# Modulation rows of a conditioned transformer block: outputs on partitions, contraction along the free axis

## The chip, the cores and the metric

One core of a Trainium2 chip runs the whole program. The metric is the device time of one execution in microseconds (us). TensorE (PE) multiplies matrices, VectorE (DVE), ScalarE (ACT) and GpSimd (POOL) work on 128 partitions of SBUF, and SyncE (SP) and ACT issue the transfers (DMAs) from DRAM.

## What is computed

A model of three blocks, all in float32, on 256 tokens of width 1024. Layers 0 and 1 are alike: a mixer (attention within a band, a short convolution, two sigmoid gates), then a gated feed-forward part of width 2816. The third block ("block 2") has a mixer of stick-breaking attention and pooling and a feed-forward part, and its norms and residual gates are modulated by six rows of 1024 numbers, which depend on nothing but a vector `c`:

```python
mod = jax.nn.silu(c) @ w_cond[l] + b_cond[l]          # (1, 1024) @ (1024, 6144)
shift_m, scale_m, gate_m, shift_f, scale_f, gate_f = jnp.split(mod, 6, axis=-1)
h = rmsnorm(x, g_mix_pre[l]) * (1.0 + scale_m) + shift_m
...
x = x + gate_m * rmsnorm(mix, g_mix_post[l])
h = rmsnorm(x, g_ffn_pre[l]) * (1.0 + scale_f) + shift_f
```

The change concerns the first line alone: a product of one row with a 1024 x 6144 matrix.

## The kernel before

All weights lie in one packed array in the order of their use (`ORDER`), in chunks of 128 x 2048 float32 (1 MB). `emit_raw` loads a chunk on SP's queue into one of four `raw` buffers, five chunks ahead of its use. `emit_split` cuts each half of it into two parts three chunks ahead: `H`, a rounded copy that ACT writes (the group CAST at L271), and `L`, the rest, that DVE writes (TENSOR_TENSOR at L272). There are nine buffers of each. PE multiplies with both parts (`mm`, L242). So each MB of weights costs two CASTs on ACT and two subtractions on DVE, while PE works on chunks split before.

24 chunks of `ORDER` hold the 1024 x 6144 matrix ("cond" chunks, four to each of the six rows). They are not split, and PE takes no part in them. `N_COND` sets where they stand: two among the chunks of `w_attn_proj` of layer 0 (the stage "ap"), nine in the feed-forward part of layer 0, four in the gates of layer 1, nine in the feed-forward part of layer 1. For each, `cond_chunk` (L490) lets DVE do two SCALAR_TENSOR_TENSOR (STT, L501) that multiply 1024 columns by one number per partition (`silu_c`) and add them to an accumulator `cacc`. The contraction lies on the partitions, so after the fourth chunk GpSimd sums over them (`partition_all_reduce`, L504), and a DMA on ACT's queue writes the row to `modd` in DRAM (L505). A new row begins with a DVE memset of `cacc` (L495) and a DMA of 4 KB that puts `b_cond` into its partition 0 (L496). The rows of `modd` are read back, broadcast to all partitions, from the end of the feed-forward part of layer 1 on (`get_rows` near L902, `gated` near L935).

`silu_c` is 128 x 8, worked out of `csb` (the vector `c`, 4 KB, loaded among the late constants) by one Sigmoid on ACT and one product on DVE. They are written behind the gates' sigmoids of the mixer (L739, L740); the scheduler of the framework, which places every instruction in its engine's queue by its own model, puts them far ahead, at 40 us.

Other names: `ga`, `gb` are the mixer's gates; `pap` is the product with `w_attn_proj`; `ptm` are PE's transposes of the gated mix (`turn`), which wait for DVE's product and sum (L753, L754); `rd`, `P` and `PTp` belong to the softmax (DVE's reciprocal, the weights that POOL scales at L643, PE's transposes of them); `dn` is the down product of a feed-forward part, `sA`, `ptf` its first blocks' gated product and the transposes of it; `xg_nm`, `pt_nm`, `xm` are the modulated, normed input of block 2's mixer, its transposes and their copies, and `p2q`, `p2k` the first products there. Buffers of 128 x 1024 float32 come from a pool of 17 (`s4`).

Of the kernel before, what the change touches and what calls it, by code (L numbers as in the profile page):

```python
# [10 lines left out]
F32 = mybir.dt.float32  # L11
F32R = mybir.dt.float32r
AF = mybir.ActivationFunctionType
ALU = mybir.AluOpType
# [4 lines left out]
P = 128  # L19
D = 1024  # L20
T = 256
KT = D // P
# [93 lines left out]
def pack_weights(inp):  # L116
    splits = dict(q=0, kv=1024, cb=1536, cc=2560, cx=3584, ga=4608, gb=5632)
    out = np.empty((len(ORDER), P, CH), np.float32)

    def put(i, w, r0, nk, c0, nc_):  # L120
        src = w[r0:r0 + nk * P, c0:c0 + nc_]
        if nk == 4:
            out[i].reshape(P, nk, nc_)[...] = src.reshape(nk, P, nc_).transpose(1, 0, 2)
        else:
            out[i].reshape(P, 2, nk, nc_ // 2)[...] = src.reshape(nk, P, 2, nc_ // 2).transpose(1, 2, 0, 3)

    for i, k in enumerate(ORDER):
        n = k[0]
        if n == "q":
            put(i, inp["w_in"][k[1]], 512 * k[3], 4, 512 * k[2], 512)  # L130
        elif n == "kv":
            put(i, inp["w_in"][k[1]], 512 * k[2], 4, 1024, 512)
        elif n in ("cc", "cx", "cb"):
            put(i, inp["w_in"][k[1]], 0, 8, splits[n] + 256 * k[2], 256)
        elif n in ("ga", "gb", "cp", "ap"):
            w = {"cp": "w_conv_proj", "ap": "w_attn_proj"}.get(n, "w_in")
            put(i, inp[w][k[1]], 512 * (k[2] % 2), 4, splits.get(n, 0) + 512 * (k[2] // 2), 512)
        elif n == "cond":
            put(i, inp["w_cond_2"][0], 256 * k[2], 2, 1024 * k[1], 1024)
        elif n in ("q2", "k2", "v2", "u2"):  # L140
            put(i, inp["w_in_2"][0], 512 * k[1], 4, 512 * ("q2", "k2", "v2", "u2").index(n), 512)
        else:
            l = k[1]
            sfx, li = ("", l) if l < 2 else ("_2", 0)
            if n == "wo":
                put(i, inp["w_out" + sfx][li], 256 * k[2], 2, 0, 1024)
            elif n == "d":
                put(i, inp["w_down" + sfx][li], 256 * k[2], 2, 0, 1024)
            elif n in ("gA", "uA"):
                w = inp[("w_gate" if n == "gA" else "w_up") + sfx][li]  # L150
                put(i, w, 512 * k[2], 4, 0, 512)
            else:
                w = inp[("w_gate" if n == "g" else "w_up") + sfx][li]
                put(i, w, 0, 8, 512 + 256 * k[2], 256)
    return out
# [3 lines left out]
def tile_model(ctx: ExitStack, tc: tile.TileContext, x_in, wpack, sink, convw, gains, c_in,  # L159
               b_cond, w_pool, pool_scale, ident_c, rope_c, amask_c, smask_c, tri_c, pmat_c, out):  # L160
    nc = tc.nc
    cst = ctx.enter_context(tc.tile_pool(name="cst", bufs=1))
# [6 lines left out]
    def s4(name, shape=(P, D), dt=F32):  # L169
        return ac.tile(list(shape), dt, tag="s4", name=name, bufs=NS4)  # L170
# [77 lines left out]
    def emit_raw():  # L248
        i = state["raw"]
        t = wp.tile([P, CH], F32, tag="raw", name=f"raw{i}", bufs=NRAW)  # L250
        n = 2 if i < 2 else 1
        for h in range(n):
            hs = slice(h * CH // n, (h + 1) * CH // n)
            state["dma"] = nc.sync.dma_start(t[:, hs], wpack[i][:, hs])
        raws[i] = t
        state["raw"] += 1

    def emit_split():
        i = state["spl"]
        while state["raw"] <= i:  # L260
            emit_raw()
        if ORDER[i][0] == "cond":
            HL[i] = raws[i]
        else:
            r = raws[i]
            hv = []
            for hf in range(2):
                H = wp.tile([P, CH // 2], F32R, tag="H", name=f"H{i}_{hf}", bufs=NSPLIT)
                L = wp.tile([P, CH // 2], F32R, tag="L", name=f"L{i}_{hf}", bufs=NSPLIT)
                rv = r[:, hf * (CH // 2):(hf + 1) * (CH // 2)]  # L270
                nc.scalar.copy(H, rv)  # L271
                nc.vector.tensor_sub(L, rv, H.bitcast(F32))  # L272
                hv.append((H, L))
            HL[i] = hv
        state["spl"] += 1

    def get(key):
        i = state["use"]
        assert ORDER[i] == key, (ORDER[i], key)
        n = len(ORDER)  # L280
        while state["raw"] < min(i + LOOK_RAW, n):
            emit_raw()
        while state["spl"] < min(i + LOOK, n):
            emit_split()
        state["use"] += 1
        return HL.pop(i)
# [22 lines left out]
    ident_r = cst.tile([P, P], F32R, tag="identr", name="ident_r")  # L309
    nc.vector.tensor_copy(ident_r, ident)  # L310
    modd = dr.tile([6, D], F32, tag="modd", name="modd")
    silu_c = cst.tile([P, KT], F32, tag="silu_c", name="silu_c")
    amask = cst.tile([P, 2, P], F32, tag="amask", name="amask")
    rope = cst.tile([P, 2, 32], F32, tag="rope", name="rope")
    negsink = cst.tile([P, DEPTH, NH], F32, tag="negsink", name="negsink")
    cw = cst.tile([P, DEPTH, KT, 3], F32, tag="cw", name="cw")
    csb = cst.tile([P, KT], F32, tag="csb", name="csb")
    pscale = cst.tile([P, 4], F32, tag="pscale", name="pscale")

    def late_consts():  # L320
        nc.sync.dma_start(rope, rope_c)
        nc.sync.dma_start(amask, amask_c)
        nc.sync.dma_start(
            negsink, sink.rearrange("l h -> (l h)").partition_broadcast(P).rearrange("p (l h) -> p l h", l=DEPTH))
        nc.vector.tensor_scalar(negsink, negsink, -1.0, None, ALU.mult)
        nc.sync.dma_start(cw, convw)
        nc.sync.dma_start(csb, c_in)
        nc.sync.dma_start(pscale, pool_scale)


# [150 lines left out]
        ch = [(get(("wo", l, j)), mp.ks(0, 2 * j, 2), mp.ks(1, 2 * j, 2)) for j in kts[lead:]]  # L481
        row_out(ch, accs, lead > 0, make_post, after)

    cacc = [None]

    def cond_due():
        while state["use"] < len(ORDER) and ORDER[state["use"]][0] == "cond":
            cond_chunk(ORDER[state["use"]])

    def cond_chunk(key):  # L490
        w = get(key).rearrange("p (h k c) -> p k h c", k=2, h=2)
        r, j = key[1], key[2]
        if j == 0:
            a = s4(f"cacc{r}")
            nc.vector.memset(a, 0.0)  # L495
            nc.scalar.dma_start(a[0:1, :], b_cond[r:r + 1, :])  # L496
            cacc[0] = a
        a = cacc[0]
        for k in range(2):
            a3 = a.rearrange("p (h c) -> p h c", h=2)  # L500
            nc.vector.scalar_tensor_tensor(a3, w[:, k], silu_c[:, 2 * j + k:2 * j + k + 1], a3, ALU.mult, ALU.add)  # L501
        if j == 3:
            mrow = s4(f"mrow{r}")
            nc.gpsimd.partition_all_reduce(mrow, a, P, bass_isa.ReduceOp.add)  # L504
            nc.scalar.dma_start(modd[r:r + 1, :], mrow[0:1, :])  # L505

    def ffn(l, xp, norms, make_post, after):
        order = [k for k in ORDER if k[0] in ("g", "u", "d") and k[1] == l]
# [164 lines left out]
    def mixer1(l, xp, norms):  # L673
# [12 lines left out]
        if l == 0:  # L686
            with tc.issue_after(state["dma"].ins):
                late_consts()
# [8 lines left out]
        for j in range(4):  # L697
            cc = s2(f"cc{l}{j}", (P, 2, T))
            mmB(f"pcc{l}{j}", get(("cc", l, j)), xp, lambda c, o: both(cc[:, c], o))
            u = ac.tile([P, 2, T + 2], F32, tag="u", name=f"u{l}{j}", bufs=1)  # L700
# [5 lines left out]
            for c in range(2):  # L706
                w = cw[:, l, 2 * j + c, :]
# [26 lines left out]
        for c in range(2):  # L734
            nc.scalar.activation(gt["ga"][c], gt["ga"][c], AF.Sigmoid)
            nc.scalar.activation(gt["gb"][c], gt["gb"][c], AF.Sigmoid)
            nc.vector.tensor_mul(yc[c], yc[c], gt["gb"][c])
            if l == 0 and c == 0:
                nc.scalar.activation(silu_c, csb, AF.Sigmoid)  # L739
                nc.vector.tensor_mul(silu_c, silu_c, csb)  # L740

# [125 lines left out]
        return mp  # L867


    xp = Pair("x0")  # L870
    norms = [Norm(t, G0, None, xp, f"n0{t}") for t in range(2)]
    norms[0].vec()
# [3 lines left out]

    for l in range(DEPTH):
        mp = mixer1(l, xp, norms)
        gpm, gpf = row(4 * l + 1, f"gpm{l}"), row(4 * l + 2, f"gpf{l}")
        xp = Pair(f"xf{l}")  # L880
# [156 lines left out]
```

## Time and profile before

| | |
|---|---|
| median of three runs | 1181.87 us (1181.78 to 1183.03) |
| the profiled execution's own time | 1181.56 us |
| its span in the profile | 1179.7 us |
| PE busy | 1145.0 us, 97% |
| DVE busy | 837.0 us, 71% |
| ACT busy | 659.6 us, 56% |
| POOL busy | 126.5 us, 11% |
| mean granted clock of TensorE | 0.948 of full speed |

The span runs from the first to the last instruction of the profiled execution; 1.86 us of its time lie around it. The profile gives for each engine what it did, for how long, and what it waited for; a wait is put down to the instruction that came last. Busy time of an engine other than PE costs something only where PE ends up waiting for it.

### The profile page before, as it was taken

To read this page: it belongs to the slowest core of one execution; us is meant where nothing else is said; L and a number is where in the kernel's file an instruction comes from. 1 tells how busy PE (TensorE), PEld (TensorE's weight loads), DVE (VectorE), ACT (ScalarE), POOL (GpSimd) and SP (SyncE) were. 2 spreads that over 40 slices of the span, in tenths; PEclk is the share of its full clock that TensorE was granted. 3 is DMA by queue.
4 is the path that set the end of the run, shared out by engine and by line. 5 is a ranking of instruction groups with operands and counts; after the bars stand their busy time and mean duration, and the time that the engine had idled before them with its cause. 6 is when DMAs were issued, how large, how long until landed. Compare 5 with 4: busy or idle time off the path is not lost.

```text
span 1179.7 us, 15598 instructions
## 1 busy us (share of the span) xinstructions
PE 1145.0 (97%) x5896; PEld 957.7 (81%) x5896; DVE 837.0 (71%) x1146; ACT 659.6 (56%) x1107; POOL 126.5 (11%) x146
## 2 busy tenths in 40 slices
PE   6999999999999999999999999999999999999997
PEld 4887888878888887887888878888887777888886
DVE  6787845769788757787757768887968448765652
ACT  5775756556555446676646455555455546655451
POOL 0011310010202001013230012020212002000000
PEclk9998999999999999999999999999999999999999
DMA  8742334756666665634447556675865345655520
GB/s 316 281 143 108 136 140 171 268 183 251 240 257 248 223 241 188 241 107 143 144 168 296 198 181 232 233 297 187 314 255 196 127 161 179 245 178 184 201 85 36
DMA packets 36243, 235.36 MB, mean 200 GB/s; under 512 B 4668, under 2 KB 5180, under 8 KB 9416
## 3 DMA queue, kind: packets, MB, share of 16 engines
q1 hardware_dynamic: 33696, 225.41, 52.7%
q10 hardware_dynamic: 2472, 8.96, 2.3%
q8 instruction: 46, 0.75, 0.3%
q14 instruction: 29, 0.24, 0.1%
HBM read 233.28 MB, written 1.07 MB: 199 GB/s over the span
## 4 chain that ended last, share of the span: by engine, by line
PE 49%; DVE 3%; POOL 2%; ACT 2%; issue 1%; POOLq 0%; DVEq 0%; ACTq 0%
PE dn L242 9%; PE pu L242 9%; PE pg L242 8%; PE wo L242 2%; PE pcp L242 2%; PE pap L242 2%; PE pgb L242 2%; PE pga L242 2%; PE puA L242 1%; PE pgA L242 1%; PE pcx L242 1%; PE z L242 1%; PE pv L242 1%; PE p2k L242 1%; PE po L242 1%
## 5 line engine op out<-in xcount | busy, mean ns | idle before, releaser
L272 DVE TENSOR_TENSOR L<-raw,H 128x1024 fp32r<-128x1024 f32 x374 | 476.7, 1284 | 178.2 <-ACT H L271 168.4
L271 ACT CAST H<-raw 128x1024 fp32r<-128x1024 f32 x374 | 390.5, 1050 | 210.3 <-issue 33.8
L242 PE MATMUL dn<-H,fHL 128*128 128x512 f32 x432 | 116.4, 391 | 0.4 <-DVE fHL L548 0.2
L242 PE MATMUL pu<-xf,H 128*128 128x512 f32 x432 | 108.2, 392 | 0.0
L242 PE MATMUL pg<-xf,H 128*128 128x512 f32 x432 | 107.8, 391 | 0.0
L242 PEld LDWEIGHTS dn<-H,fHL 128*128 128x128 f32 x432 | 79.8, 188 | 16.7 <-ACT fHL L547 0.6
L242 PEld LDWEIGHTS pg<-xf,H 128*128 128x128 f32 x432 | 79.2, 188 | 15.2
L242 PEld LDWEIGHTS pu<-xf,H 128*128 128x128 f32 x432 | 77.7, 189 | 13.9
L643 POOL TENSOR_SCALAR P<-P,rd 128x256 f32<-128x256 f32 x64 | 46.9, 750 | 228.2 <-ACT cc L428 107.6
L242 PE MATMUL dn<-L,fHL 128*128 128x512 f32 x216 | 67.1, 390 | 0.0
L242 PEld LDWEIGHTS pg<-xf,L 128*128 128x128 f32 x432 | 58.9, 190 | 4.2
L242 PEld LDWEIGHTS pu<-xf,L 128*128 128x128 f32 x432 | 58.9, 190 | 4.2
L504 POOL PARTITION_ALL_REDUCE mrow<-cacc x6 | 38.9, 6486 | 217.4 <-DMA raw<-in_wpack_dram 177.4
L501 DVE SCALAR_TENSOR_TENSOR cacc<-raw,silu_c,cacc 128x1024 f32<-128x1024 f32 x48 | 61.3, 1277 | 0.2
L242 PE MATMUL pu<-xf,L 128*128 128x256 f32 x432 | 60.2, 282 | 0.0
L242 PE MATMUL pg<-xf,L 128*128 128x256 f32 x432 | 60.2, 282 | 0.0
L242 PE MATMUL wo<-H,m 128*128 128x512 f32 x192 | 52.5, 394 | 0.0
L547 ACT CAST fHL<-f 128x512 fp32r<-128x512 f32 x27 | 16.7, 620 | 57.3 <-DVE f L545 57.3
L242 PEld LDWEIGHTS dn<-L,fHL 128*128 128x128 f32 x216 | 40.6, 188 | 8.5
L242 PEld LDWEIGHTS wo<-H,m 128*128 128x128 f32 x192 | 35.6, 188 | 7.2 <-issue 0.2
L636 ACT ACTIVATE P<-S,nm 128x256 f32<-128x256 f32 x64 | 29.4, 473 | 12.2 <-DVE nm L630 12.2
L541 ACT ACTIVATE s<-s 128x512 f32<-128x512 f32 x27 | 17.1, 632 | 33.1 <-DVE s L429 33.1
(277 smaller groups left out, 2006.4 us busy)
## 6 DMA issues: line engine op xcount, KB each, us to landing
raw<-in_wpack_dram SPq DMA_DIRECT2D x209, 1024.0 KB, 4.9
raw<-in_wpack_dram SPq DMA_DIRECT2D x4, 512.0 KB, 8.8
gpm<-in_gains_dram ACTq DMA_DIRECT2D x3, 512.0 KB, 7.4
gpf<-in_gains_dram ACTq DMA_DIRECT2D x3, 512.0 KB, 8.0
gqf<-in_gains_dram ACTq DMA_DIRECT2D x2, 512.0 KB
out_dram<-x SPq DMA_DIRECT2D x4, 256.0 KB, 2.1
pmat<-in_pmat_dram SPq DMA_DIRECT2D x2, 384.0 KB, 5.5
x<-in_x_dram SPq DMA_DIRECT2D x2, 256.0 KB, 2.6
```

The lines of the kernel that those rows point to most:

```text
L242: nc.tensor.matmul(o, a, b, start=start, stop=stop, **kw)
L271: nc.scalar.copy(H, rv)
L272: nc.vector.tensor_sub(L, rv, H.bitcast(F32))
L501: nc.vector.scalar_tensor_tensor(a3, w[:, k], silu_c[:, 2 * j + k:2 * j + k + 1], a3, ALU.mult, ALU.add)
L504: nc.gpsimd.partition_all_reduce(mrow, a, P, bass_isa.ReduceOp.add)
L541: last = nc.scalar.activation(s, s, AF.Silu)
L547: nc.scalar.copy(fHL[:, 0], fv)
L636: nc.scalar.activation(Pt[:, hh, :], S[hh // 2][:, hh % 2, :], AF.Exp, bias=nm[:, hh:hh + 1], accum_out=den[:, hh:hh + 1])
L643: nc.gpsimd.tensor_scalar(Pt[:, hh, :], Pt[:, hh, :], rd[:, hh:hh + 1], 0.0, ALU.mult, ALU.add)
```

## The change

The weights of a cond chunk are packed the other way round: partition p holds the eight outputs 8p to 8p+7 of a row, two of them per chunk, each with all its 1024 weights along the free axis. An STT multiplies them by `silu_c`, now the whole vector on each partition (128 x 1024), and its accumulating output writes the sum over the free axis into one column of `mcol`. The product itself goes back into the `raw` buffer, and nobody reads it. After four chunks one small addition adds the bias `bcol` (128 x 6 x 8, loaded among the late constants in place of the old `csb`), and the DMA to `modd` takes 32 bytes from each partition. The six sums over partitions, six memsets and six bias DMAs go. `csb` becomes a broadcast of `c` to 128 partitions, 512 KB, issued on ACT's queue behind the gate's sigmoid in layer 0, and Sigmoid and product that make `silu_c` are now 128 x 1024. Two ACT_TABLE_LOADs are no longer in ACT's queue: the one ahead of the old, early Sigmoid of `silu_c`, and the one ahead of the first softmax exponential.

```diff
         elif n == "cond":
-            put(i, inp["w_cond_2"][0], 256 * k[2], 2, 1024 * k[1], 1024)
+            w = inp["w_cond_2"][0][:, 1024 * k[1]:1024 * (k[1] + 1)].reshape(D, P, KT)
+            out[i].reshape(P, 2, D)[...] = w[:, :, 2 * k[2]:2 * k[2] + 2].transpose(1, 2, 0)
...
-    silu_c = cst.tile([P, KT], F32, tag="silu_c", name="silu_c")
+    mcol = cst.tile([P, 6, KT], F32, tag="mcol", name="mcol")
+    bcol = cst.tile([P, 6, KT], F32, tag="bcol", name="bcol")
...
-        nc.sync.dma_start(csb, c_in)
+        nc.sync.dma_start(bcol, b_cond)
...
     def cond_chunk(key):
-        w = get(key).rearrange("p (h k c) -> p k h c", k=2, h=2)
+
+        w = get(key).rearrange("p (u k) -> p u k", u=2)
         r, j = key[1], key[2]
-        if j == 0:
-            a = s4(f"cacc{r}")
-            nc.vector.memset(a, 0.0)
-            nc.scalar.dma_start(a[0:1, :], b_cond[r:r + 1, :])
-            cacc[0] = a
-        a = cacc[0]
-        for k in range(2):
-            a3 = a.rearrange("p (h c) -> p h c", h=2)
-            nc.vector.scalar_tensor_tensor(a3, w[:, k], silu_c[:, 2 * j + k:2 * j + k + 1], a3, ALU.mult, ALU.add)
+        for u in range(2):
+            nc.vector.scalar_tensor_tensor(w[:, u], w[:, u], 1.0, silu_c, ALU.mult, ALU.mult,
+                                           accum_out=mcol[:, r, 2 * j + u:2 * j + u + 1])
         if j == 3:
-            mrow = s4(f"mrow{r}")
-            nc.gpsimd.partition_all_reduce(mrow, a, P, bass_isa.ReduceOp.add)
-            nc.scalar.dma_start(modd[r:r + 1, :], mrow[0:1, :])
+            nc.vector.tensor_add(mcol[:, r], mcol[:, r], bcol[:, r])
+            nc.scalar.dma_start(modd[r].rearrange("(p j) -> p j", p=P), mcol[:, r])
...
             if l == 0 and c == 0:
+                csb = s4("csb")
+                nc.scalar.dma_start(csb, c_in[0].partition_broadcast(P))
                 nc.scalar.activation(silu_c, csb, AF.Sigmoid)
                 nc.vector.tensor_mul(silu_c, silu_c, csb)
...
+    silu_c = s4("silu_c")
```

The scheduler places the changed instructions anew, and some others with them. Line numbers of the changed kernel differ by a few from those of before. Three places matter here.

DVE in the stage "ap" of layer 0, where the first two cond chunks are used. The row of `ga` with `pap` is the product that the first `ptm` needs, the next `ga` row the sum behind it. Before:

```order
L272 TENSOR_TENSOR L_1_2083<-raw_2059,H_1_2082 128x1024
L272 TENSOR_TENSOR L_0_2154<-raw_2069,H_0_2153 128x1024
L501 SCALAR_TENSOR_TENSOR cacc_2071<-raw_1925,silu_c,cacc_2071 128x1024
L272 TENSOR_TENSOR L_1_2158<-raw_2069,H_1_2157 128x1024
L501 SCALAR_TENSOR_TENSOR cacc_2071<-raw_1925,silu_c,cacc_2071 128x1024
L272 TENSOR_TENSOR L_0_2166<-raw_2076,H_0_2165 128x1024
L501 SCALAR_TENSOR_TENSOR cacc_2071<-raw_1997,silu_c,cacc_2071 128x1024
L753 TENSOR_TENSOR ga_1568<-pap_2086,ga_1568 128x512
L501 SCALAR_TENSOR_TENSOR cacc_2071<-raw_1997,silu_c,cacc_2071 128x1024
L754 TENSOR_TENSOR ga_1568<-ga_1568,yc_1564 128x512
```

and with the change:

```order
L273 TENSOR_TENSOR L_1_2083<-raw_2062,H_1_2082 128x1024
L273 TENSOR_TENSOR L_0_2154<-raw_2072,H_0_2153 128x1024
L735 TENSOR_TENSOR silu_c<-silu_c,csb 128x1024
L273 TENSOR_TENSOR L_1_2158<-raw_2072,H_1_2157 128x1024
L494 SCALAR_TENSOR_TENSOR raw_1926,mcol<-raw_1926,silu_c 128x1024 x2
L494 SCALAR_TENSOR_TENSOR raw_1998,mcol<-raw_1998,silu_c 128x1024
L748 TENSOR_TENSOR ga_1569<-pap_2086,ga_1569 128x512
L494 SCALAR_TENSOR_TENSOR raw_1998,mcol<-raw_1998,silu_c 128x1024
L749 TENSOR_TENSOR ga_1569<-ga_1569,yc_1565 128x512
L273 TENSOR_TENSOR L_0_2166<-raw_2076,H_0_2165 128x1024
```

One STT is still ahead of each of the two `ga` rows, the product for `silu_c` stands ahead of an `L` and of all STTs, and three `L` rows stand differently. ACT in the same place, with the change:

```order
L725 COPY ga_1570<-pga_2000 128x512
L733 DMA csb<-in_c_dram 128x1024
L272 CAST H_1_2082<-raw_2062 128x1024
L272 CAST H_0_2153<-raw_2072 128x1024
L734 ACTIVATE silu_c<-csb 128x1024
L272 CAST H_1_2157<-raw_2072 128x1024
L725 COPY ga_1570<-pga_2026 128x512
L728 ACTIVATE ga_1570<-ga_1570 128x1024
```

The load of `csb` follows the copy of a gate, and the Sigmoid of `silu_c` stands between two CASTs; before, the small DMA into `cacc` and the same CASTs stood here. On PE the first `ptm` follows one matmul of its group of four with the change, where it followed three.

PE at the end of the feed-forward part of layer 1, where block 2's input is transposed (`pt_nm`) among the last `dn` products. Before:

```order
L242 MATMUL dn_11_6831<-H_1_7844,fHL_7684 128x512 x4
L242 MATMUL dn_11_6831<-L_1_7845,fHL_7684 128x512 x2
L242 MATMUL dn_11_6831<-H_1_7859,fHL_7825 128x512 x4
L242 MATMUL dn_11_6831<-L_1_7860,fHL_7825 128x512
L377 MATMUL pt_nm_8008<-ident,xg_nm_7958 128x128 x4
L242 MATMUL dn_11_6831<-L_1_7860,fHL_7825 128x512
L377 MATMUL pt_nm_8025<-ident,xg_nm_7958 128x128 x4
L242 MATMUL p2q_8129<-H_0_7865,xm_8013 128x512
L242 MATMUL p2k_8156<-H_0_8091,xm_8013 128x512
```

and with the change:

```order
L243 MATMUL dn_11_6818<-L_1_7815,fHL_7523 128x512 x2
L378 MATMUL pt_nm_7987<-ident,xg_nm_7937 128x128 x4
L243 MATMUL dn_11_6818<-H_1_7824,fHL_7664 128x512
L378 MATMUL pt_nm_8004<-ident,xg_nm_7937 128x128 x4
L243 MATMUL dn_11_6818<-H_1_7824,fHL_7664 128x512 x3
L243 MATMUL dn_11_6818<-L_1_7825,fHL_7664 128x512 x2
L243 MATMUL dn_11_6818<-H_1_7838,fHL_7805 128x512 x4
L243 MATMUL dn_11_6818<-L_1_7839,fHL_7805 128x512 x2
L243 MATMUL p2q_8108<-H_0_7844,xm_7992 128x512 x4
```

The first `pt_nm` stands 12 matmuls ahead of the last `dn` ones instead of one. On DVE the two halves of `x` and of `xg_nm` there start ahead of three `L` rows, which they followed before.

DVE at the first softmax unit of layer 0 (`y` is the low part of the convolution's gated output). Before:

```order
L272 TENSOR_TENSOR L_1_801<-raw_600,H_1_800 128x1024
L272 TENSOR_TENSOR L_0_864<-raw_689,H_0_863 128x1024
L639 TENSOR_TENSOR den_638<-den_638,es_636 128x4
L641 RECIPROCAL rd_646<-den_638 128x4
L208 TENSOR_TENSOR y_685<-yc_592,y_685 128x2x256
L429 TENSOR_TENSOR cc_688<-pcc_0_699,cc_688 128x256
```

and with the change:

```order
L273 TENSOR_TENSOR L_1_802<-raw_601,H_1_801 128x1024
L273 TENSOR_TENSOR L_0_865<-raw_690,H_0_864 128x1024
L632 TENSOR_TENSOR den_639<-den_639,es_637 128x4
L209 TENSOR_TENSOR y_686<-yc_593,y_686 128x2x256
L634 RECIPROCAL rd_647<-den_639 128x4
L430 TENSOR_TENSOR cc_689<-pcc_0_700,cc_689 128x256
```

The reciprocal `rd`, for which POOL waits, stands behind `y` now.

## Rows read from the trace of the kernel before

**Rows 1.** Page, part 1: busy us of each engine, share of the span, instructions.
```profile
PE 1145.0 (97%) x5896; PEld 957.7 (81%) x5896; DVE 837.0 (71%) x1146; ACT 659.6 (56%) x1107; POOL 126.5 (11%) x146
```

**Rows 2.** Waits of PE: tile, line, releaser: us in total, times, longest us.
```profile
PE PTp L651 <- POOL P L643: 5.9, 6, 1.2
```

**Rows 3.** Lines of DVE by form: busy us, mean ns | idle before.
```profile
L272 DVE TENSOR_TENSOR L<-raw,H 128x1024 fp32r<-128x1024 f32 x374 | 476.7, 1284 | 178.2 <-ACT H L271 168.4 <-PE pcx L242 1.3 <-PE pcc L242 0.5
L501 DVE SCALAR_TENSOR_TENSOR cacc<-raw,silu_c,cacc 128x1024 f32<-128x1024 f32 x48 | 61.3, 1277 | 0.2
...
L404 DVE SCALAR_TENSOR_TENSOR x<-ag_pm,rs_apm,x 128x512 f32<-128x512 f32 x12 | 8.9, 747 | 1.2 <-POOL rs_apm L345 1.2
...
L495 DVE MEMSET cacc<- 128x1024 f32 x6 | 5.5, 912 | 1.0 <-issue 1.0
```

**Rows 4.** Page, part 5: GpSimd's sum over partitions.
```profile
L504 POOL PARTITION_ALL_REDUCE mrow<-cacc x6 | 38.9, 6486 | 217.4 <-DMA raw<-in_wpack_dram 177.4
```

**Rows 5.** Timeline, 713 to 727 us: start, us, engine, instruction [idle before, releaser].
```profile
713.06 6.13 POOL L504 PARTITION_ALL_REDUCE mrow<-cacc  x1 [7.09 <-PE pgA L242]
...
713.38 6.42 DVE L272 TENSOR_TENSOR L<-raw,H 128x1024 fp32r<-128x1024 f32 x2 [1.05 <-ACT H L271]
...
720.33 5.75 DVE L272 TENSOR_TENSOR L<-raw,H 128x1024 fp32r<-128x1024 f32 x5
...
720.97 1.05 ACT L271 CAST H<-raw 128x1024 fp32r<-128x1024 f32 x1 [0.32 <-PE puA L242]
...
726.01 0.68 DVE L531 TENSOR_TENSOR sA<-puA,sA 128x512 f32<-128x512 f32 x1
...
726.74 0.66 PE L516 MATMUL ptf<-ident,sA 128*128 128x128 f32 x4 [1.28 <-DVE sA L531]
```

**Rows 6.** Timeline, 211 to 226 us, all engines.
```profile
211.13 0.59 ACT L732 COPY ga<-pga 128x512 f32<-128x512 f32 x1 [1.39 <-PE pga L242]
...
217.20 1.06 ACT L735 ACTIVATE ga<-ga 128x1024 f32<-128x1024 f32 x1
...
222.61 0.68 DVE L753 TENSOR_TENSOR ga<-pap,ga 128x512 f32<-128x512 f32 x1
...
224.41 0.68 DVE L754 TENSOR_TENSOR ga<-ga,yc 128x512 f32<-128x512 f32 x1
...
225.24 0.63 PE L746 MATMUL ptm<-ident,ga 128*128 128x128 f32 x4
```

**Rows 7.** Timeline, 866 to 872 us: one row of gains loaded on ACT's queue.
```profile
866.85 0.36 ACTq L294 DMA_DIRECT2D gqf<-in_gains_dram  x1
...
870.18 0.19 ACT L337 ACTIVATION_READ_ACCUMULATOR jk_apf<-dn 128x1 f32 x1
...
871.24 0.69 DVE L397 TENSOR_TENSOR ag_pf<-dn,gqf 128x512 f32<-128x512 f32 x1 [3.05 <-DMA gqf<-in_gains_dram]
```

**Rows 8.** DMA issues, a 512 KB row of gains on ACT's queue: KB, median us to landing.
```profile
gpf<-in_gains_dram ACTq DMA_DIRECT2D x3, 512.0 KB, 8.0
```

**Rows 9.** Timeline, 883 to 897 us: end of the second feed-forward part.
```profile
883.09 1.07 PE L242 MATMUL dn<-H,fHL 128*128 128x512 f32 x4
...
886.81 0.63 PE L377 MATMUL pt_nm<-ident,xg_nm 128*128 128x128 f32 x4 [1.06 <-DVE xg_nm L368]
...
889.44 0.96 PE L242 MATMUL p2q<-H,xm 128*128 128x512 f32 x3 [0.81 <-DVE xm L208]
...
896.52 0.66 PE L377 MATMUL pt_nm<-ident,xg_nm 128*128 128x128 f32 x4 [0.44 <-DVE xg_nm L368]
```

**Rows 10.** Timeline, 69 to 75 us: first softmax unit of layer 0.
```profile
69.68 1.28 ACT L636 ACT_TABLE_LOAD   x1
...
73.69 0.66 DVE L208 TENSOR_TENSOR y<-yc,y 128x512 fp32r<-128x512 f32 x1
```

**Rows 11.** Windows: busy us of PE, PEld, DVE, ACT, POOL (x instructions), PEclk, DMA.
```profile
340.00:360.00 20.00, 20.00 (x110) 17.31 (x109) 18.68 (x22) 10.40 (x16) 0.35 (x1) 0.95 0.92 357
100.00:120.00 20.00, 20.00 (x120) 16.85 (x119) 14.12 (x32) 11.25 (x29) 2.83 (x4) 0.88 0.27 102
```

More of the change, by code (lines that the diff above doesn't have):

```diff
@@ L316, in tile_model @@
     cw = cst.tile([P, DEPTH, KT, 3], F32, tag="cw", name="cw")
-    csb = cst.tile([P, KT], F32, tag="csb", name="csb")
     pscale = cst.tile([P, 4], F32, tag="pscale", name="pscale")
@@ L482, in mix_out @@
         row_out(ch, accs, lead > 0, make_post, after)
-    cacc = [None]
     def cond_due():
@@ L1018 @@
         ("gains", np.stack(g)),
-        ("c", inp["c_2"].reshape(KT, P).T),
-        ("b_cond", inp["b_cond_2"].reshape(6, D)),
+        ("c", inp["c_2"].reshape(1, D)),
+        ("b_cond", inp["b_cond_2"].reshape(6, P, KT).transpose(1, 0, 2)),
         ("w_pool", inp["w_pool_2"][0].transpose(1, 0, 2)),
```

## The prediction

> **What bounds the kernel now.** The page's first part comes first: PE is busy for 1145.0 of 1179.7 us, DVE for 71% and POOL for 11% [rows 1]. So only what makes PE wait costs time, and only PE's 34.7 idle us can be won. The list of PE's waits says next who ends them. Two of its entries bear on this change at most: what DVE delivers late, and what POOL delivers late in the softmax, 5.9 us in six waits of at most 1.2 [rows 2]. POOL's sums over partitions, 6 of 6.5 us [rows 4], are in that list nowhere. Then I read DVE's groups by shape for the prices [rows 3] and the timeline at the places where instructions move. Of a stage without PE idle, the window from 340 to 360 us is the densest on DVE: 18.68 of 20 us busy, and PE still at 20.00 [rows 11].
>
> The profiled execution took 1181.56 us; the sum is made against that. The median of the runs is 0.31 us above it, which I add at the end. A measurement of this kernel can tell a difference of about 0.2%, 2.4 us, from none.
>
> **What costs or gives nothing.** The six memsets go, 5.5 us of DVE [rows 3]. So does what the sums over partitions do to DVE. While one ran from 713.06 to 719.19, DVE's two subtractions took 6.42 us, where five took 5.75 a little later [rows 5]: 2 x 1.15 = 2.3, so 4.1 us are lost. Six times that is some 25 us, an upper estimate, 3% of DVE's busy time. DVE gains some 30 us of room in all and PE nothing of it, except where a result was late (B below); the split parts are made three chunks ahead, and that stock covers delays of this size already. In the other direction each of the 48 STTs writes an accumulator. No row shows that on DVE. The nearest is ACT's own read of one, 0.19 us [rows 7]; I take 0.1 of DVE for each, between nothing and 0.19, some 5 us altogether, covered by the same stock. The reads of c and of the bias, the small additions and the writes to DRAM are off PE's path: the rows are read back from the end of the second feed-forward part on, and a row's write no longer waits for a sum of 6.5 us. SP's queue keeps its order: a small load takes the place of a small load. The weight bytes are the same, and in-place STTs free a raw buffer when the old ones did.
>
> **A, the load of c at the stage "ap": +0.8.** The first STT now needs 512 KB that are issued where the first mixer ends. The copy of the gate at 211.13 [rows 6] is just ahead of the issue, so the load starts at about 211.2. A row of gains of that size, issued on the same queue at 866.85, let its reader start at 871.24, after 4.4 us [rows 7]; the median of three others is 8.0 [rows 8]. I take 4.4, the only single load of this kind whose issue and reader I can follow in the timeline. Then: data at 215.6; Sigmoid of 128 x 1024, 1.06 as the gate's [rows 6], to 216.7; product on DVE, 1.25 as a subtraction of that size [rows 3], to 217.9; a subtraction, which stands next, to 219.05; three STTs of 1.3 (1.2 from start to start, 224.41 − 222.61 less the 0.6 of the product between [rows 6], and 0.1 for the accumulator) to 222.95; product with `pap` to 223.55; the fourth STT to 224.85; the sum to 225.5. Before, that sum ran from 224.41 and PE came to `ptm` at 225.24 without a wait [rows 6]. Now `ptm` stands two matmuls earlier, at 2 x 0.227 (six take 1.36) = 0.45 before, 224.8. So PE waits for about 0.8. Bounds: 0, as nothing waited here that could be won, and 0.8 + 3.6 = 4.4 if the load takes 8.0.
>
> The small gaps of the CASTs on ACT around the new Sigmoid are hidden: PE works on parts split before, and ACT has 44% free.
>
> **B, the one late result behind a sum over partitions: −1.3.** The stretched subtractions from 713.38 push five others together until `sA` comes at 726.01, and PE's `ptf` waits 1.28 [rows 5]. Without the stretch the last of the five is bound by ACT's part, which was there at 720.97 + 1.05 = 722.0, so it is done by 723.3, and `sA` by 723.9, ahead of PE's arrival at 725.46. The whole wait goes. Bounds −1.3 and 0. What is late next: nothing that I find in that stretch.
>
> **C, end of the second feed-forward part: −0.6.** Here PE waits 1.06, 0.81 and 0.44, in all 2.31 [rows 9]. With the change the first transposes stand 11 matmuls earlier, where PE arrives at about 883.1 [rows 9]. DVE's `x` and `xg_nm` are moved ahead of three subtractions there, and I place the end of their chain (norm on ACT and POOL included) at about 885.0, so PE waits 1.9 once. After that 12 `dn` matmuls (2.7 us) cover the copies for which `p2q` waited, and that wait is gone. Then the second transposes: from 886.81 to PE's arrival at 896.08 it worked 9.27 − 0.81 = 8.46, and 11 matmuls more take 2.5: 885.0 + 8.46 + 2.5 = 895.96 instead of 896.52. Bounds: −2.3, if the chain is early enough for no wait at all, and +1.9, if the new wait comes and the old ones stay.
>
> **D, first softmax unit of layer 0: +0.4.** The table load of 1.28 on ACT goes, but den on DVE stood behind subtractions, not behind ACT. The reciprocal now comes after `y`, 0.66 [rows 10], so POOL starts 0.66 later, and PE's transposes follow; part of it is covered by other matmuls. A later unit changes in the same way. I take +0.4. Bounds: −1.2, the longest wait of that kind, if ACT was the limit after all [rows 2], and 2 x 0.66 = +1.3.
>
> In 100 to 120 us the granted clock is 0.88 against 0.95 elsewhere [rows 11]; 20 x (1 − 0.88/0.95) = 1.5 us that a shifted softmax can move either way.
>
> **Sum.** 0.8 − 1.3 − 0.6 + 0.4 = −0.7: 1180.9 for a profiled execution, **1181.2** for the median.
>
> **Rivals.** *An STT with an accumulating output runs at half rate* (slower). Per column an STT costs (1277 − 747)/512 = 1.035 ns [rows 3], that is 1.06 us more for 1024. Three stand ahead of the sum for `ptm`: A grows by 3.2. Where DVE has 18.68 of 20 us busy [rows 11] the two of a chunk come late once more, 2.1, unless the room from B's stretch covers it. 1181.2 + 3.2 + 2.1 = 1186.5; with A alone 1184.4. It decides if such an STT takes over 2 us. For it: no row has one. Against it: STTs with two float32 operands from SBUF take 1.035 ns a column now. Chance 0.12. The Trainium skill ("Vector Engine (DVE) Microarchitecture Reference", "Points that are easy to get wrong") says just this of an STT: two sources in SBUF that are not bf16 halve its throughput, as no read port is left for the accumulator. The STTs before have two such sources and take 1.035 ns a column, hardly more than the subtractions' 1284 ns for 1024, so the trace does not agree for them; with the accumulator no run here shows it.
>
> *The load of c is as slow as the median row* (slower): 8.0 instead of 4.4, 1181.2 + 3.6 = 1184.8. For it: weights fill the queues at times, 0.92 of the DMA engines at 340 us [rows 11]. Against it: the one load that I could follow took 4.4. Chance 0.07.
>
> *All waits go* (faster): B −1.3, C −2.3, D −1.2, A 0: 1181.56 − 4.8 + 0.31 = 1177.1. For it: DVE has 30 us more room, and every term's wait ends on DVE. Against it: POOL and ACT stand in the chains of C. Half of it is enough to count as faster. Chance 0.2.
>
> *Nothing reaches PE*: the waits are replaced by others of the same size, 1181.9. That the sums over partitions hardly show in PE's waits is for it, B against it. Chance 0.13.
>
> **How the numbers follow.** Forecast 0.48, half rate 0.12, slow load 0.07, all waits gone 0.2, nothing 0.13. Forecast and "nothing" are within 0.2% (1179.5 to 1184.2): same 0.61; faster 0.2; slower 0.19. The range reaches from 1178.0, which holds part of the fast case, to 1186.0, which holds the slow load and the half rate with A alone.
>
> **What would show it.** Right: the STT group at 1.3 to 1.4 us mean; the subtractions' mean near 1.22 us instead of 1.284; no wait of `ptf` near 726 us; a wait of `ptm` near 225 us of about 0.8; one wait of `pt_nm` near 884 us of about 1.9. Wrong: STTs over 2 us; PE waits for `L`; a wait at `ptm` of over 3 us; other new waits in PE's list that sum to more than 2 us.

## The result, and the profile after

The changed kernel takes 1185.41 us (median of 20 runs, 1179.84 to 1187.18), the kernel before in the runs beside them 1181.49 (20 runs, 1179.33 to 1185.02). The ratio on record is 1.0027, 95% interval 1.0018 to 1.0035: slower by 3.2 us (3.9 by the two medians) where 0.7 us less was forecast (1181.2 against 1181.87), inside the range, on the side that had a chance of 0.19. Timed again beside the experiments it gave 1.0007 (0.9996 to 1.0017), which is not told from equal. So it is 0.3% slower in one timing and at most 0.2% in the other, and single executions of it spread over 7 us; what the record shows of both is below.

The profiled execution took 1184.12 us. The page's first part:

```profile
span 1182.3 us, 15617 instructions
...
PE 1145.0 (97%) x5896; PEld 959.7 (81%) x5896; DVE 810.9 (69%) x1194; ACT 660.2 (56%) x1105; POOL 88.9 (8%) x140
```

DVE lost 26.1 us of work and POOL 37.6, as the change promised [rows 1], and the span is 2.6 us longer. The groups of DVE by shape:

```profile
L273 DVE TENSOR_TENSOR L<-raw,H 128x1024 fp32r<-128x1024 f32 x374 | 455.9, 1225 | 202.9 <-ACT H L272 191.0 <-PE pcc L243 2.1 <-PE pcx L243 1.3
L494 DVE SCALAR_TENSOR_TENSOR raw<-raw,silu_c 128x1024 f32<-128x1024 f32 x48 | 58.3, 1221 | 3.3 <-DMA raw<-in_wpack_dram 3.1
```

The subtractions are back at 1225 ns, 20.8 us less in all than with the sums over partitions, and an STT with an accumulating output is no slower than the old ones [rows 3]: 1221 ns, and a read of the accumulator of 0.08 us that the timelines below show. The largest growth in PE's list of waits (in total, times, longest) is here:

```profile
PE PTp L644 <- POOL P L636: 9.0, 8, 2.1
```

`ptf` behind `sA` and `p2q` behind `xm` are gone from it. The waits for POOL's softmax scaling grew from 5.9 to 9.0 us [rows 2]; the longest of them, 2.14, lies in layer 0 (D, below), where it takes the place of two others, and most of the growth is in layer 1. The windows say where, with the window that stood in [rows 11] ahead of them:

```profile
340.00:360.00 20.00, 20.00 (x112) 17.40 (x111) 13.90 (x19) 10.83 (x16) 0.00 (x0) 1.00 0.75 276
520.00:540.00 20.00, 17.89 (x106) 14.47 (x105) 15.18 (x35) 12.16 (x33) 5.35 (x8) 0.91 0.45 158
580.00:600.00 20.00, 16.46 (x79) 13.47 (x78) 12.55 (x21) 9.67 (x22) 8.60 (x7) 0.91 0.42 144
```

and the last of these in the kernel before:

```profile
580.00:600.00 20.00, 19.06 (x100) 15.27 (x101) 10.34 (x17) 10.19 (x21) 4.74 (x5) 0.95 0.39 153
```

In the attention of layer 1 PE is 2.6 us less busy in the last window, POOL is busy for 8.60 us instead of 4.74, and in two windows the granted clock is 0.91 where the window from 340 us has 1.00. (The profiled execution of the kernel before shows 0.95 in nearly all windows; its matmuls take the same time, so that level costs nothing here.) By these rounded shares 20 x (1 − 0.91) / 0.5 = 3.6 us of each such window ran at half clock, 1.2 GHz; the table below shows 1.4 us lost by the first of them.

PE executes the same 5896 matmuls in almost the same order in all these kernels, so the start of the n-th can be compared. The shift against the profiled execution of before, in us, at the matmul that starts there at the time given:

| at (before) | changed | what lies between |
|---|---|---|
| 71.9 | +0.58 | the start: first loads |
| 114.0 | −0.13 | softmax of layer 0 (D) |
| 222.7 | −0.50 | the load of c (A) comes just here |
| 272.1 | −0.49 | A is past |
| 504.5 | −0.56 | |
| 535.2 | −0.08 | |
| 577.3 | +1.28 | half clock at 536 |
| 595.0 | +5.62 | last softmax units of layer 1 |
| 723.4 | +5.46 | |
| 728.2 | +3.97 | `sA` (B) |
| 862.6 | +3.97 | |
| 904.8 | +2.69 | end of the second feed-forward part (C) |
| 1169.7 | +2.16 | |

The whole loss, 6.2 us, falls between 504 and 595 us, in a stretch that the prediction does not mention. Of it 0.5 comes at 511 us, where PE now waits 0.39 for POOL's `P`, 1.4 with the half clock at 536, and 4.3 from 577.3 on.

### The profile page after: what moved, and what is told of

Same layout as the page of the kernel before. It is cut to its first block, busy times and chain, and to the rows that moved or that the text cites. A ratio compares the mean times of both kernels' runs of the same rounds, so it can differ in the third digit from the quotient of the medians.

```text
span 1182.3 us, 15617 instructions
## 1 busy us (share of the span) xinstructions
PE 1145.0 (97%) x5896; PEld 959.7 (81%) x5896; DVE 810.9 (69%) x1194; ACT 660.2 (56%) x1105; POOL 88.9 (8%) x140
## 4 chain that ended last, share of the span: by engine, by line
PE 49%; DVE 3%; POOL 2%; ACT 2%; issue 1%; POOLq 0%; DVEq 0%; ACTq 0%
PE dn L243 10%; PE pu L243 10%; PE pg L243 8%; PE wo L243 2%; PE pap L243 2%; PE pga L243 2%; PE pgb L243 2%; PE puA L243 2%; PE pgA L243 1%; PE pcx L243 1%; POOL P L636 1%; PE z L243 1%; PE pcp L243 1%; PE pv L243 1%; PE p2k L243 1%
## 5 line engine op out<-in xcount | busy, mean ns | idle before, releaser
L273 DVE TENSOR_TENSOR L<-raw,H 128x1024 fp32r<-128x1024 f32 x374 | 455.9, 1225 | 202.9 <-ACT H L272 191.0
L636 POOL TENSOR_SCALAR P<-P,rd 128x256 f32<-128x256 f32 x64 | 50.5, 806 | 229.8 <-DVE rd L634 102.6
L494 DVE SCALAR_TENSOR_TENSOR raw<-raw,silu_c 128x1024 f32<-128x1024 f32 x48 | 58.3, 1221 | 3.3 <-DMA raw<-in_wpack_dram 3.1
```

The costliest lines, as they stand in the source:

```text
L494: nc.vector.scalar_tensor_tensor(w[:, u], w[:, u], 1.0, silu_c, ALU.mult, ALU.mult, accum_out=mcol[:, r, 2 * j + u:2 * j + u + 1])
L636: nc.gpsimd.tensor_scalar(Pt[:, hh, :], Pt[:, hh, :], rd[:, hh:hh + 1], 0.0, ALU.mult, ALU.add)
```

## The experiments

Each was timed in five rounds beside the kernel before, whose median was 1181.91 beside the first four, 1182.55 beside the next three and 1182.57 beside the last two; the table has all nine. The ratios are those on record and differ from the ratios of the medians by up to 0.0007.

| kernel | median, us | ratio to before, 95% interval |
|---|---|---|
| changed, again | 1183.61 | 1.0007 (0.9996 to 1.0017) |
| changed, layer 0's order as before | 1185.07 | 1.0025 (1.0015 to 1.0035) |
| before, layer 0's order as changed | 1181.18 | 0.9995 (0.9986 to 1.0003) |
| before without the sums | 1179.95 | 0.9988 (0.9978 to 0.9999) |
| changed, two STTs behind the last `rd` | 1181.99 | 0.9996 (0.9986 to 1.0005) |
| changed, one of them behind it | 1183.96 | 1.0011 (0.9999 to 1.0023) |
| before, two STTs let through early | 1187.98 | 1.0047 (1.0030 to 1.0065) |
| changed, two STTs behind the last `o` | 1179.48 | 0.9979 (0.9969 to 0.9988) |
| the same, layer 0's order as before | 1180.38 | 0.9982 (0.9974 to 0.9991) |

**Is it the order in layer 0's softmax, or chance?** My first theory blamed D's place. It was tried in both directions, beside a second look at the changed kernel and the kernel before without the sums.

Changed kernel, no edit:

> The changed kernel once more, for a second trace of it. The trace shown lost its time in half-clock stretches of 3.4 us each (three, where the kernel before had one), two of them in the attention of layer 1, where the order of no engine was changed. Theory 1 (the new order in the softmax of layer 0 causes them): about 1185, over the kernel before by 3 to 4 us, the first stretch again in layer 0. Theory 2 (the rest of the change causes them): the same time. Theory 3 (where they fall is chance from run to run): a time between 1180 and 1187, and stretches at other places than in the first trace.

Changed kernel with the early table loads back:

```diff
+    ssm = cst.tile([P, KT], F32, tag="ssm", name="ssm")
...
             if l == 0 and c == 0:
                 csb = s4("csb")
                 nc.scalar.dma_start(csb, c_in[0].partition_broadcast(P))
+                nc.scalar.activation(ssm, bcol[:, 0], AF.Sigmoid)
+                nc.vector.tensor_mul(ssm, ssm, bcol[:, 0])
                 nc.scalar.activation(silu_c, csb, AF.Sigmoid)
```

> The changed kernel with a small Sigmoid and product of 128 x 8 put back where silu_c was worked out before (on the bias, into a tile that nobody reads), so that ACT's two table loads are back at 40 and 70 us and the order of DVE and ACT in the attention of layer 0 is that of before again; all else is as changed. Theory 1 (order in the softmax of layer 0): 1180 to 1181.5, as B and C gain and no stretch is added. Theory 2 (the rest of the change): 1185. Theory 3 (chance): its runs spread as those of the changed kernel do.

Kernel before without its early Sigmoid:

```diff
-                nc.scalar.activation(silu_c, csb, AF.Sigmoid)
-                nc.vector.tensor_mul(silu_c, silu_c, csb)
+                nc.vector.tensor_mul(silu_c, csb, csb)
```

> The kernel before without the Sigmoid of silu_c (it becomes c times c, so the modulation rows have other values): the two table loads go, and DVE and ACT take the changed kernel's order in the attention of layer 0, nothing else is moved. Theory 1 (order in the softmax of layer 0): 1184 to 1186. Theory 2 (the rest): 1181.5, as before. Theory 3 (chance): as before within the spread of its runs.

Kernel before without the sums:

```diff
-            mrow = s4(f"mrow{r}")
-            nc.gpsimd.partition_all_reduce(mrow, a, P, bass_isa.ReduceOp.add)
-            nc.scalar.dma_start(modd[r:r + 1, :], mrow[0:1, :])
+            nc.scalar.dma_start(modd[r:r + 1, :], a[0:1, :])
```

> The kernel before without GpSimd's sums over partitions (the row is written from partition 0 of the accumulator, so the modulation rows lack the other partitions' parts). The order of the attention in layer 0 stays that of before; the end of the second feed-forward part takes nearly the changed kernel's order. Theory 1 (order in the softmax of layer 0): 1179.5, by B -1.5 and C -1.3 as the traces of the two kernels show them. Theory 2 (the sums' going causes the stretches): 1183 to 1186. Theory 3 (chance): 1179 to 1185.

Theory 1 fell: with layer 0's order undone the changed kernel is as slow as ever, and with that order alone the kernel before is not slower. The sums' going gains 1.4 us by itself (0.9988, whose interval ends at 0.9999), in the direction of B and C, so it is not the cause either. Chance plays its part: the second trace of the changed kernel has no half clock in layer 1, and shifts of −0.32 at 504.5 and 0.00 at 577.3. But from 577.3 to 595.0 it still loses 2.86 us (the changed kernel's first trace 4.3, the one with layer 0's order undone 4.1, the two made from the kernel before −0.01 and 0.00). Something there belongs to the change. The timeline of that second trace, DVE, POOL and PE in 577 to 597 us:

```profile
578.80 1.28 DVE L494 SCALAR_TENSOR_TENSOR raw<-raw,silu_c 128x1024 f32<-128x1024 f32 x1
580.01 0.08 DVE L494 DVE_READ_ACCUMULATOR raw<-raw,silu_c 128x1 f32 x1
...
587.54 1.22 DVE L494 SCALAR_TENSOR_TENSOR raw<-raw,silu_c 128x1024 f32<-128x1024 f32 x1
...
588.68 0.16 DVE L623 SCALAR_TENSOR_TENSOR nm<-m,negsink 128x4 f32<-128x4 f32 x1
...
577.00 5.42 POOL L636 TENSOR_SCALAR P<-P,rd 128x256 f32<-128x256 f32 x4 [5.52 <-DVE rd L634]
591.56 4.95 POOL L636 TENSOR_SCALAR P<-P,rd 128x256 f32<-128x256 f32 x4 [9.13 <-ACT yc L723]
...
580.48 0.33 PE L644 MATMUL PTp<-ident,P 128*128 128x128 f32 x1 [0.82 <-POOL P L636]
582.48 0.55 PE L644 MATMUL PTp<-ident,P 128*128 128x128 f32 x3 [1.67 <-POOL P L636]
...
596.56 0.55 PE L644 MATMUL PTp<-ident,P 128*128 128x128 f32 x3 [1.09 <-POOL P L636]
```

and the kernel before at the same place:

```profile
576.95 3.93 POOL L643 TENSOR_SCALAR P<-P,rd 128x256 f32<-128x256 f32 x4 [5.70 <-DVE rd L641]
588.97 3.86 POOL L643 TENSOR_SCALAR P<-P,rd 128x256 f32<-128x256 f32 x4 [8.08 <-ACT yc L730]
...
580.94 0.55 PE L651 MATMUL PTp<-ident,P 128*128 128x128 f32 x3 [1.15 <-POOL P L643]
```

Two STTs that the kernel before does not have here. The first lies beside POOL's four scalings of `P`, which take 5.42 us instead of 3.93, and PE's transposes wait for them for 2.49 us instead of 1.15. The second stands ahead of `nm`, for which ACT's exponentials wait; POOL starts the last unit 2.6 us later than before, 1.6 of which PE has lost already at 582.9 us. POOL's four scalings then take 4.95 us instead of 3.86, and PE waits 1.09 where it did not wait.

DVE's order says why they are there; the first expectation above is wrong in holding that no engine's order had changed in the attention of layer 1. These are the first two STTs of row 3 (chunk 0). The changed kernel, in the last units of layer 1:

```
L209 TENSOR_TENSOR o_5452<-po_5443,o_5452 128x2x256
L494 SCALAR_TENSOR_TENSOR raw_5627,mcol<-raw_5627,silu_c 128x1024
L430 TENSOR_TENSOR cb_5393<-pcb_1_5435,cb_5393 128x256
...
L620 TENSOR_REDUCE m_5529<-S_5528 128x2
L494 SCALAR_TENSOR_TENSOR raw_5627,mcol<-raw_5627,silu_c 128x1024
L623 SCALAR_TENSOR_TENSOR nm_5542<-m_5529,negsink 128x4
```

In the kernel before they stand some 20 rows later, behind the row's memset, after the attention:

```
L495 MEMSET cacc_5790 128x1024
...
L501 SCALAR_TENSOR_TENSOR cacc_5790<-raw_5635,silu_c,cacc_5790 128x1024
```

The accumulator came from the pool of 17 buffers. My reading is that the memset stood so late because the softmax's tiles held these buffers; the experiment with a buffer of its own, below, bears it out. The accumulator that the change removes, whose memset comes ahead of its STTs, had kept them out of the softmax. That is theory 4. Theory 5 is that STTs of the new kind hurt wherever they stand.

**Moving only these two STTs.** The changed kernel with both queued behind the last unit's reciprocal (`state["rd"]`, the instruction that computes `rd`), and with the first alone:

```diff
         for u in range(2):
-            nc.vector.scalar_tensor_tensor(w[:, u], w[:, u], 1.0, silu_c, ALU.mult, ALU.mult,
-                                           accum_out=mcol[:, r, 2 * j + u:2 * j + u + 1])
+            late = (r, j) == (3, 0) and u in (0, 1)
+            with tc.issue_after(state["rd"].ins) if late else nullcontext():
+                nc.vector.scalar_tensor_tensor(w[:, u], w[:, u], 1.0, silu_c, ALU.mult, ALU.mult,
+                                               accum_out=mcol[:, r, 2 * j + u:2 * j + u + 1])
...
-            nc.vector.reciprocal(rd, den)
+            state["rd"] = nc.vector.reciprocal(rd, den)
```

> The changed kernel with one thing kept back: on DVE the two STTs of the chunk (row 3, j 0) are queued behind the reciprocal of layer 1's last softmax unit; in the changed kernel one stood in the unit before it and one ahead of nm of the last, in the kernel before both behind the last. No other engine's order moves. Theory 4 (these two places cost 2.7 us of PE in 577 to 597 us, and half-clock stretches now and then): 1179 to 1180.5, no new wait of PTp at 577 to 597. Theory 5 (STTs with an accumulating output, written in place, are what hurts, wherever they stand, as by holding POOL up): 1184 to 1185.5 as the changed kernel.

With `u in (0,)`:

> As the last, but only one of the two STTs is queued behind the reciprocal: one still stands beside POOL's scaling of P in the last unit but one, none stands ahead of nm. Theory 4: about half of the 2.7 us comes back, 1.3 to 1.5 us by PTp's wait near 582 us, so 1181 to 1182. Theory 5: as the changed kernel.

And the converse, the kernel before with `cacc` of row 3 in a buffer of its own:

```diff
+    cacc3 = cst.tile([P, D], F32, tag="cacc3", name="cacc3")
...
-            a = s4(f"cacc{r}")
+            a = cacc3 if r == 3 else s4(f"cacc{r}")
```

> The kernel before with a buffer of its own for the accumulator of row 3, whose memset and bias row waited for a free buffer of the pool before. With that alone its two first STTs, of the old kind, move to the very places that they have in the changed kernel (one in the last softmax unit but one, one ahead of nm of the last). Theory 4: 2.7 us and more over the kernel before, 1184 to 1186, PTp waits in 577 to 597 us as in the changed kernel. Theory 5: no difference to the kernel before, 1181.9.

The converse decides between the theories. With that one buffer DVE takes the changed kernel's order at this place, old STTs, memsets, sums and all, and the time goes up by 0.47%. Its PE has the same waits:

```profile
580.24 0.33 PE L652 MATMUL PTp<-ident,P 128*128 128x128 f32 x1 [0.84 <-POOL P L644]
582.23 0.55 PE L652 MATMUL PTp<-ident,P 128*128 128x128 f32 x3 [1.66 <-POOL P L644]
...
596.31 0.55 PE L652 MATMUL PTp<-ident,P 128*128 128x128 f32 x3 [1.11 <-POOL P L644]
```

From 577.3 to 595.0 its trace loses 2.86 us, as the changed kernel's second one does. Theory 5 is out. Its median lies above the 1184 to 1186 that was expected, and not all of the 0.47% comes from the STTs in the softmax: this trace loses another 2.2 us between 877 and 904.8 us, where the load of `scl_m` lands 8.1 us after its issue (5.8 in the kernel before), PE waits 3.31 us for `xg_nm` instead of 1.06, and a stretch at half clock follows.

The two STTs behind `rd` were a miss of 1.5 us by my own expectation: 1181.99. The wait at 582 us went (shift −1.21 at 577.3, −1.19 at 582.9), but from there to 595.0 a new one of 3 us came. DVE, POOL and PE in that trace:

```profile
587.52 1.19 DVE L496 SCALAR_TENSOR_TENSOR raw<-raw,silu_c 128x1024 f32<-128x1024 f32 x1
...
588.64 1.22 DVE L496 SCALAR_TENSOR_TENSOR raw<-raw,silu_c 128x1024 f32<-128x1024 f32 x1
...
589.79 5.01 DVE L273 TENSOR_TENSOR L<-raw,H 128x1024 fp32r<-128x1024 f32 x4
...
587.77 7.75 POOL L638 TENSOR_SCALAR P<-P,rd 128x256 f32<-128x256 f32 x4 [8.10 <-ACT yc L725]
...
592.65 0.55 PE L646 MATMUL PTp<-ident,P 128*128 128x128 f32 x3 [0.39 <-POOL P L638]
595.12 1.00 PE L646 MATMUL PTp<-ident,P 128*128 128x128 f32 x4 [1.92 <-POOL P L638]
```

Directly behind `rd` the STTs and four subtractions run without a gap, and POOL needs 7.75 us for what takes 4 x 0.48 = 1.9 alone. So it is not only late DVE results: DVE's work beside POOL's stretches it. Over the kernel before's 64 scalings (minimum, median, maximum in ns):

```profile
L643 POOL TENSOR_SCALAR P<-P,rd x64: 472/481/2500, 74.0 to 590.3; 128x256 f32<-128x256 f32 x64
```

By a straight-line fit over the 64 of the changed kernel's second trace, one scaling takes 0.43 us plus 0.80 us for each us of overlap with a DVE instruction that has two operands in SBUF (`L`, the STTs, `qs`, `yc`, `y`, the product `u`); the 29 without overlap take 0.48, none over 0.51. Instructions with one operand in PSUM (`o`, `cc`, `cb`) get 0.0 to 0.2 in a joint fit over all eleven traces. The Trainium skill ("SBUF — State Buffer", "Who interferes with whom") says this as a rule: a DVE instruction with two inputs in SBUF contends with a GpSimd instruction that reads SBUF, since both use one shared port. The traces agree. That the sums over partitions are what stretched the subtractions beside them [rows 5] is shown by the kernel before without the sums, whose subtractions take 1225 ns where the kernel before has 1284; that the port is the way in which they do it would fit, but no run tests it by itself.

With one STT still beside POOL (behind `rd` only the other), the median is 1183.96 where 1181 to 1182 was expected: a miss, with an interval that tells it from neither neighbour, 1.0007 and 0.9996. Its trace has the waits of 0.83 and 1.67 near 582 us unchanged, and the moved STT now lies beside POOL's last four scalings, which take 6.60 us there, so the hoped-for gain could not come. It also has three stretches at half clock.

**Behind POOL's last scaling.** The same edit with another anchor, `state["at"]`, the instruction that writes the low part of the last attention output `o`:

```diff
-                nc.vector.tensor_sub(self.ks(1, k0 + a, m)[:, :, ts_], sr, h.bitcast(F32))
+                state["at"] = nc.vector.tensor_sub(self.ks(1, k0 + a, m)[:, :, ts_], sr, h.bitcast(F32))
...
+        with tc.issue_after(state["at"].ins) if (r, j) == (3, 0) else nullcontext():
...
```

> The changed kernel with the two STTs of the chunk (row 3, j 0) queued on DVE behind the low part of the last attention output (o), 2 subtractions and more after POOL's last scaling of P. DVE's order through the whole attention of layer 1 is then that of the kernel before. Theory 4, as the run with the STTs behind the reciprocal has refined it (a DVE instruction with two operands in SBUF holds POOL's scaling up for as long as both overlap, 0.8 us per us): the wait of 3.1 us that stood near 592 us goes, B and C stay, 1179 to 1180.5, 2 to 3 us under the kernel before. Rival: the STTs make L of the gates late instead, PE waits for L near 600 us, 1182 and more.

With the early table loads of the second experiment as well:

> The last kernel with the small early Sigmoid and product put back as well, so that DVE's and ACT's order in the attention of layer 0 is that of before too. Theory 4: within 1 us of the last kernel, 1179 to 1181, as the order in layer 0 gave or cost at most 0.7 us in the traces so far. Rival (the early table loads hold something up now): 1182 and more.

1179.48 us, 0.9979 of the kernel before (0.9969 to 0.9988): faster than both kernels. POOL, PE and the first of the two STTs in its trace:

```profile
575.62 3.88 POOL L638 TENSOR_SCALAR P<-P,rd 128x256 f32<-128x256 f32 x4 [5.53 <-DVE rd L636]
587.59 3.86 POOL L638 TENSOR_SCALAR P<-P,rd 128x256 f32<-128x256 f32 x4 [8.10 <-ACT yc L725]
...
579.55 0.55 PE L646 MATMUL PTp<-ident,P 128*128 128x128 f32 x3 [1.09 <-POOL P L638]
591.81 1.03 PE L646 MATMUL PTp<-ident,P 128*128 128x128 f32 x8
...
598.74 1.22 DVE L496 SCALAR_TENSOR_TENSOR raw<-raw,silu_c 128x1024 f32<-128x1024 f32 x1
```

The softmax is as in the kernel before, from 577.3 to 595.0 nothing is lost (the shift goes from −1.39 to −1.41), and PE's list has no wait for `L` that would pay for it. Putting layer 0's order back on top gives 1180.38, a difference within the spread: the medians do not tell what that order costs or gives; the traces do (D, below).

## Why the prediction was wrong

**The step that failed** is "What costs or gives nothing": "The six memsets go, 5.5 us of DVE" and "DVE gains some 30 us of room in all and PE nothing of it". The room was about right (26.1 us), but the memset was costed as busy time alone. The accumulator that it opens was also a gate: the STTs of its row could not start before the memset, and the memset stood where the pool had a buffer for it. The kernel before with a buffer of its own keeps the memset and loses the gate, with the same 2.86 us. With the gate gone the scheduler put two STTs into the last softmax units of layer 1, 2.9 us of PE by the second trace. This place was in the order of DVE to be read, a fourth one beside the three that I followed, and none of the rivals names it; only the last sign of being wrong, other new waits of more than 2 us, covers it. On PE's own queue nothing moves in layer 1's attention.

**A, the load of c, +0.8:** 0.0. The mechanism ran as described, in smaller steps:

```profile
210.65 0.39 ACTq L733 DMA_DIRECT2D csb<-in_c_dram  x1
...
214.17 1.06 ACT L734 ACTIVATE silu_c<-csb 128x1024 f32<-128x1024 f32 x1 [0.21 <-DMA csb<-in_c_dram]
...
223.27 0.69 DVE L749 TENSOR_TENSOR ga<-ga,yc 128x512 f32<-128x512 f32 x1
...
224.27 0.60 PE L741 MATMUL ptm<-ident,ga 128*128 128x128 f32 x4
```

The load took 3.5 us, not 4.4, and STTs start 1.15 apart with their accumulator's read, not 1.3. The sum ends at 223.96 and PE comes at 224.27 without a wait. The rival of a slow load falls with it. (The prediction's own steps give 225.5 − 224.8 = 0.7, not 0.8.)

**B, `sA`, −1.3:** −1.5 (3.97 − 5.46). `sA` is done ahead of PE, which goes through without a wait:

```profile
728.66 0.68 DVE L524 TENSOR_TENSOR sA<-puA,sA 128x512 f32<-128x512 f32 x1
```

```profile
730.76 0.60 PE L509 MATMUL ptf<-ident,sA 128*128 128x128 f32 x4
```

**C, end of the second feed-forward part, −0.6:** −1.3 (2.69 − 3.97). One wait of 2.12 instead of three of together 2.31 [rows 9], where 1.9 was forecast:

```profile
888.54 0.63 PE L378 MATMUL pt_nm<-ident,xg_nm 128*128 128x128 f32 x4 [2.12 <-DVE xg_nm L369]
...
899.24 0.66 PE L378 MATMUL pt_nm<-ident,xg_nm 128*128 128x128 f32 x4
```

0.8 of it came earlier, by 877 us, in the down products; the kernel before without the sums gains the same 0.8 there, so it comes with the sums' going. The prediction does not have it. From there to 904.8 us, the place that it describes, 0.5 was gained where 0.6 was forecast.

**D, first softmax unit, +0.4:** −0.7 from 71.9 to 114.0, a difference of two larger steps. The delay that was forecast came, and was larger: by 78.6 us the changed kernel has lost 3.8, half clock included (the kernel before with that order alone 3.4). `rd` came 0.5 later, as forecast within 0.2. But with the table load gone ACT's CASTs come earlier too, and two subtractions run beside POOL's scalings, which take 4.10 us instead of 2.33:

```profile
75.39 2.56 DVE L273 TENSOR_TENSOR L<-raw,H 128x1024 fp32r<-128x1024 f32 x2
...
75.02 4.10 POOL L636 TENSOR_SCALAR P<-P,rd 128x256 f32<-128x256 f32 x4 [55.14 <-DVE rd L634]
...
78.27 1.81 PE L644 MATMUL PTp<-ident,P 128*128 128x128 f32 x7 [2.14 <-POOL P L636]
```

Two waits of the kernel before are gone in return, at the third unit:

```profile
97.26 0.33 PE L651 MATMUL PTp<-ident,P 128*128 128x128 f32 x1 [0.70 <-POOL P L643]
98.67 1.86 PE L651 MATMUL PTp<-ident,P 128*128 128x128 f32 x7 [1.09 <-POOL P L643]
```

So "a later unit changes in the same way" was wrong. The net of −0.6 to −0.7 is in five of the six traces with the new order of layer 0 (the sixth, which has no half clock there, gains 2.2), and the four others with the old order show +0.1. The clock's part did not change the sum: both kernels run one stretch at half clock in layer 0, in [rows 11] between 100 and 120 us, in the changed kernel 20 us earlier:

```profile
80.00:100.00 20.00, 20.00 (x124) 16.98 (x123) 15.15 (x35) 12.18 (x32) 3.52 (x6) 0.94 0.29 100
```

**The sum** of A to D was −0.7 by forecast, 0.0 − 1.5 − 1.3 − 0.7 = −3.5 by the trace: the gains were forecast too small and A's cost did not come, and the kernel with the two STTs moved shows them, 2.5 us under the kernel before by its ratio (0.9979). Against them stand the softmax of layer 1, +2.9 for the two STTs and +0.5 at 511 us, and the half clock, which in the profiled execution fell there twice for some 1.5 us each. The two errors have opposite signs, and the total shows only their difference.

**The rivals.** Half rate of the accumulating STT: no, 1221 ns. The Trainium skill's rule on it ("Vector Engine (DVE) Microarchitecture Reference", "Points that are easy to get wrong") does not show in this form: two float32 sources in SBUF with an accumulating output take 1221 ns, the STTs without one 1277 [rows 3]; what two sources of another type would take, no run here shows. "All waits go" was nearer the truth for B to D in size than the forecast, and the kernel with the STTs moved ended 1179.48, on that side; as a mechanism it did not happen, for PE still waits 2.12 at C and 2.14 at D.

**What stays open.** Which waits send PE to half clock. The changed kernel's two traces have the same waits of PE near 582 and 597 us; the first has half clock there and at 536, the second, but for the program's last microseconds, in layer 0 alone. Its runs go from 1179.84 at a mean granted clock of 0.997 to 1187.15 at 0.993 and 1187.18 at 0.994, so the spread is at least in part of that kind. The waits and the half clock do go together over many runs: the kernels with an STT in layer 1's last softmax unit but one have a mean granted clock of 0.9943 to 0.9958 over their timed runs, all others of the experiments, with the kernel before beside them, 0.9964 to 0.9971. Why one execution has such a stretch and the next has not stays open. That its ratio moved from 1.0027 to 1.0007 between the two timings is not explained beyond it. Why PE waits 0.39 for POOL at 511 us, for a shift of +0.5 between 504.5 and 514.5 us in every kernel here that has no sums over partitions, was not followed.

## What to carry to other kernels

An instruction that is removed may have been a gate: ask what could not start before it, and read the new order for the instructions that it lets through, over the whole program and above all where another engine's chain ends PE's waits. Bulk work on DVE with two operands in SBUF stands badly beside a short GpSimd chain that PE waits for; queue it behind the chain, not merely behind DVE's own last part in it. And where a change moves the time little, compare the start of the same matmul in both traces: gains of 3.5 us and losses of 6 us stood here side by side in a total of 2.6.

## What was new about the hardware

An STT with an accumulating output over 1024 float32 columns from two operands in SBUF takes 1.22 us, and a separate read of the accumulator of 0.08 us follows it; started back to back they come 1.15 us apart. POOL's scaling of 128 x 256 takes 0.48 us alone and up to 2.50 beside DVE's subtractions.
